# Second feed-forward layer of a hybrid decoder step: gate and up in seven block products

## The chip, the core and the metric

The kernel runs on one core of a Trainium2 chip. The metric is device time in microseconds (us) of one execution, the median of several runs. TensorE (PE) multiplies matrices out of SBUF into PSUM, VectorE (DVE) and ScalarE (ACT) work on both memories, GpSimd (POOL) on SBUF, and SP issues most DMAs. PE's weight loads are shown apart (PEld).

## What is computed

One inference step of a two-layer decoder trunk for 512 prompt tokens and 8 x 8 sample tokens, 576 columns in all: layer 0 is dilated attention, layer 1 an S5 state-space layer (SSM) with a gated output projection (GLU). A feed-forward layer follows each. Only the second feed-forward layer is changed:

```python
def rmsnorm(x, g):
    y = x * rsqrt(mean(x * x, -1) + 1e-6)
    return y * g

def swiglu(h, w_gate, w_up, w_down):          # 1024 -> 2816 -> 1024, float32
    return (silu(h @ w_gate) * (h @ w_up)) @ w_down

x = x + swiglu(rmsnorm(x, norm_ffn[1]), ffn_w_gate[1], ffn_w_up[1], ffn_w_down[1])
```

## The kernel before

Activations are held transposed in `xT`: 8 tiles of 128 features by 576 tokens, the tokens in two halves of 288 (`HN`), each half in a PSUM bank of its own. Float32 products are made of three rounded ones: every operand is split into a high part and the rest (`whi`/`wlo` for weights, `xgh`/`xgl` for activations, `hh`/`hl` for the hidden layer), and `mm6` (L105) issues high x high, high x rest and rest x high for both halves of the tokens, six matmuls of 128 x 288.

`ffn` (L1003) runs for both layers. The hidden width goes in three thirds of 4, 4 and 3 block columns of 256 (`THIRDS`). In a block column, `gemm` loads gate weights in two chunks of 512 KB, splits each (`split_w`, L96: `whi` by ScalarE at L99, `wlo` by VectorE at L100) and accumulates 96 matmuls into two of three rotating PSUM tiles (`acc`, two banks each). VectorE scales by `nin.r`, the inverse norm of each token (L1034), ScalarE takes silu (L1035), GpSimd scales again for the up factor (L1036). Then the same for up; VectorE multiplies (L1041) and the product is split into `hh` and `hl` (L173, L174). After a third, four down projections follow, each added to `xT` (L1057). The last third of the second layer also writes the outputs.

`fetch_w` (L85) issues a weight load on SP's queue into one of four `raw` buffers, and `pace(rate)` (L78) adds `rate` (`RF` = 0.72) to a credit; for each whole credit SP also issues one copy of an old cache to its output, DRAM to DRAM (`o_kv_s<-cache_kv_w`, up to 1020 KB). These copies depend on nothing.

`Norm` (L182) prepares a layer's input: `add(m)` splits feature tile m times its gain (L178, L179) and sums the squares on ScalarE and GpSimd (L193, L194); `finish` sums over the partitions with a matmul by ones (L199), and forms `rstd` on ScalarE and VectorE (L203 to L213). The products with gate and up use the unscaled split, so they can start before `rstd` is there. The GLU of the SSM phase (`glu`, L1564 on) calls `add` for two tiles after each of its four rounds (yt at L1610, xT at L1612).

A scheduler orders the instructions of each engine; each engine runs its own in that order, and an instruction that waits holds up those behind it. In the first layer a generator (`fill`) adds the set-up of the SSM phase between matmuls: its matrices go through DRAM scratch (`e_scr`, `w_scr`, `t_scr`, `v_scr`).

Of the kernel before, what the change touches and what calls it, by code (L numbers as in the profile page):

```python
# [18 lines left out]
D = 1024  # L19
# [13 lines left out]
KST = 6  # L33
RF = 0.72
CHUNKS = ((0, 2), (1, 2), (2, 2), (0, 1), (1, 1), (0, 0), (1, 0), (2, 0), (2, 1))
# [5 lines left out]
def dram(ap, off, dims):  # L41
    return bass.AP(tensor=ap.tensor, offset=ap.offset + off, ap=[list(d) for d in dims])
# [8 lines left out]
def _build(nc, tc, A, es):  # L51
# [100 lines left out]
    xT = xp.tile([128, KT, NT], F32, name="xT")  # L152
    xg = es.enter_context(pool("xg", bufs=8))
    accp = [es.enter_context(tc.tile_pool(name=f"acc2{i}", bufs=1, space=PSUM)) for i in range(3)]
# [8 lines left out]
    aux = es.enter_context(tc.tile_pool(name="aux2", bufs=1, space=PSUM))  # L163
    nrm = es.enter_context(pool("nrm"))
    scn = {"W": scr.tile([8, 128, 2, 4, 128], F32, name="w_scr"), "V": scr.tile([8, 2, 64, 4, 2, 128], F32, name="v_scr"),
# [16 lines left out]
    class Norm:  # L182
# [4 lines left out]
        def add(self, m):  # L187
            self.x[m] = split(self.xs, xT[:, m, :], gm[:, self.gi, m:m + 1], "xgh", "xgl", self.perm)
            if m == 0:
                s.activation(self.ss, xT[:, m, :], AF.Square)  # L190
            else:
                sq = nrm.tile([128, NT], F32, name="sq")
                s.activation(sq, xT[:, m, :], AF.Square)  # L193
                g.tensor_tensor(self.ss, self.ss, sq, OP.add)  # L194

        def finish(self):
# [15 lines left out]
            else:  # L212
                v.scalar_tensor_tensor(self.r, t, 1.5, self.r, op0=OP.add, op1=OP.mult)  # L213

    n0 = Norm(1)
    with ExitStack() as p3:
# [9 lines left out]
    n1 = Norm(2, perm=True)  # L226
    ffn(nc, tc, A, L, 0, n0, n1, ssm)
    n1.finish()
    with ExitStack() as p4:
        n2 = ssm_phase(nc, tc, A, p4, L, n1, sp)  # L230
    ecx.close()
    n2.finish()
    ffn(nc, tc, A, L, 1, n2, None, None)
    assert not shifts

# [766 lines left out]

def ffn(nc, tc, A, L, layer, nin, nout, fill):  # L1003
    v, s, g, te = nc.vector, nc.scalar, nc.gpsimd, nc.tensor
    ident, pool, xT, load_w, mm6, acc, aux = (L[x] for x in ("ident", "pool", "xT", "load_w", "mm6", "acc", "aux"))
    lw = lambda n: dram(A[n], layer * D * FF, [[1, D * FF]])

# [16 lines left out]
    with ExitStack() as es:  # L1024
        hp = es.enter_context(pool("hp", bufs=9))
        wk = es.enter_context(pool("wkf", bufs=2))
        for c0, c1 in THIRDS:
# [15 lines left out]
            for c in range(4):  # L1043
                ks = range(2 * c0, 2 * c1)
                done = c1 == 11 and nout is None
                if done and c == 3:
                    ps = [acc() for _ in range(3)]
                    ws = [load_w(lw("ffn_w_down"), D, k, min(4, 2 * c1 - k), c * 256, 256) for k in ks[::4]]
                else:
                    ps, ws = gemm(lw("ffn_w_down"), D, ks, c * 256, h), None  # L1050
                for m in range(2):
                    if ws is not None:
# [3 lines left out]
                    xv = xT[:, 2 * c + m, :].rearrange("p (a b) -> p a b", a=2)  # L1056
                    v.tensor_tensor(xv, ps[m][:, :, :HN], xv, OP.add)  # L1057
                    if c1 == 11 and nout is not None:
                        nout.add(2 * c + m)
                    if not done:  # L1060
                        continue
                    if m == 0 or c == 3:
                        w = 128 if c == 3 else 256
                        yo = wk.tile([128, 4, w], F32, name="yo")
                        ys = wk.tile([64, w], F32, name="ys")
# [11 lines left out]
        if fill is not None:  # L1077
            for _ in fill:
                pass

# [315 lines left out]
def ssm_phase(nc, tc, A, es, L, nin, sp):  # L1396
    v, s, g, te = nc.vector, nc.scalar, nc.gpsimd, nc.tensor
    ident, pool, xT, fetch_w, split_w, mm6, acc, aux, scn, xg = (L[x] for x in ("ident", "pool", "xT", "fetch_w", "split_w", "mm6", "acc", "aux", "scn", "xg"))
    Ar, Ai, E63, rho, x0, xs0, KC, consts_in, consts_out = (sp[x] for x in ("Ar", "Ai", "E63", "rho", "x0", "xs0", "KC", "consts_in", "consts_out"))
    wk = es.enter_context(pool("wks", bufs=2))  # L1400
    kp = es.enter_context(pool("kps"))
    zm = kp.tile([128, 64], F32, name="zm")
    g.memset(zm, 1.0)
# [19 lines left out]
    def stage1(c, mid=None, at=(1, 0)):  # L1423
# [12 lines left out]
        for m in range(2):  # L1436
            f = 2 * c + m
            u = wk.tile([128, 2, HN], F32, name="yt", bufs=2)
            v.tensor_tensor(u, ps[m][:, :, :HN], nin.r, OP.mult)
            nc.sync.dma_start(scn["U"][f], u.rearrange("p h x -> p (h x)"))  # L1440
# [91 lines left out]
    def states():  # L1532
# [8 lines left out]
        g.tensor_tensor(fs[:, 1], t1, t2, OP.add)  # L1541
        u12 = wk.tile([128, 2, 8, 32], F32, name="R", bufs=1)
        u1, u2 = u12[:, 0], u12[:, 1]
        a8r, a8i = (x[:, 8:9, :].to_broadcast([128, 8, 32]) for x in (Ar, Ai))
        for sgn, ri, (p, q) in ((OP.subtract, 0, ((a8r, x0[:, 0]), (a8i, x0[:, 1]))), (OP.add, 1, ((a8r, x0[:, 1]), (a8i, x0[:, 0])))):
# [3 lines left out]
            g.tensor_tensor(Ss[:, ri], Ss[:, ri], u1, OP.add)  # L1549
        fo = wk.tile([32, 128, 2], F32, name="fo", bufs=1)  # L1550
        so = wk.tile([128, 2, 128, 2], F32, name="ys")
        pt = aux.tile([128, 2, 512], F32, name="aux")
# [9 lines left out]
        nc.sync.dma_start(dram(A["o_st_s"], 0, [[256, 128], [32768, 2], [1, 256]]), so.rearrange("p h a r -> p h (a r)"))  # L1562

    def glu(c0):  # L1564
# [14 lines left out]
    def glu_first():  # L1579
# [5 lines left out]
        for m in range(2):  # L1585
# [3 lines left out]
            if m == 0:  # L1589
                stage3(7)  # L1590
        gsplit(4, ("ys", 7), ("Xt", 7))
        sp["es"].close()
        N[0] = L["Norm"](3, L["es"].enter_context(L["right"]("xg2", bufs=8)))
        w = [(ps, *split_w(W2[c0][1])) for ps, c0 in ((pg, D), (pv, 0))]
# [6 lines left out]
    for c in range(4):  # L1601
        pg, pv = glu_first() if c == 0 else (glu(D + c * 256), None)
        sg = []
        for m in range(2):
            t = wk.tile([128, 2, HN], F32, name="yt", bufs=2)
            s.activation(t, pg[m][:, :, :HN], AF.Sigmoid)
            sg.append(t)
# [59 lines left out]


# [14 lines left out]
```

## Time and profile before

| what | value |
|---|---|
| time, median of 3 runs | 1490.38 us (1488.93 to 1492.78) |
| span of the profiled execution | 1486.7 us |
| median less that span | 3.7 us |
| PE, PEld busy | 98%, 92% of the span |
| DVE, ACT, POOL busy | 60%, 35%, 23% |
| matmuls | 12662 |
| first feed-forward layer | about 401 to 870 us |
| SSM phase with GLU | about 870 to 1067 us |
| second feed-forward layer | about 1067 to 1487 us |

The page gives no time of its own for the profiled execution, only its span, from the first to the last instruction; what lies around it is in the medians. Rows of groups read: line, engine, operation, output<-inputs, shapes, count, then total busy us and mean ns of one, then the idle time before them and who ended it. Rows of stretches read: stretch, its length, then for PE, PEld, DVE, ACT and POOL the busy us and in brackets the instructions, then the granted clock of TensorE, the mean busy share of the DMA engines and GB/s. Rows of the chain of waits read: start, length, engine, tile, line. Rows of waits read: who waited for whom, us in total, times, longest. Rows of DMAs read: transfer, issuing queue, count, size, median us from issue to landing.

### The profile page before, as it was taken

Reading aid. Unit: us, or ns where it says so; the run is one execution under the profiler, and the core shown is the slowest. Engines: PE = TensorE matmul, PEld = TensorE weight load, DVE = VectorE, ACT = ScalarE, POOL = GpSimd, SP = SyncE. Lnnn points to the kernel's source line nnn. Section 1 sums busy time; section 2 is a strip of 40 time slices with the busy share of each in tenths; the row PEclk is TensorE's granted clock in tenths of the full one; section 3 lists DMA queues with packets and bytes.
Section 4 is the critical chain, followed back from the end, with each engine's and each line's share of the span. In section 5 each row is a group of like instructions: output and inputs, shape, how many; then the busy total and the mean of one; then the engine's idle time right before and its main releaser. Section 6 shows DMA issues by size and latency. Waiting matters only on the chain.

```text
span 1486.7 us, 30078 instructions
## 1 busy us (share of the span) xinstructions
PE 1457.7 (98%) x12662; PEld 1370.9 (92%) x12662; DVE 896.0 (60%) x1507; ACT 526.8 (35%) x814; POOL 335.4 (23%) x393
## 2 busy tenths in 40 slices
PE   9999999999999999999999999799999999999998
PEld 7888777777899999999999999699999999999998
DVE  6898989645669545778676668745433333333342
ACT  4534455465552211332223444333422222211222
POOL 2022232310030174354444321301111000100100
PEclk9999999999999999999999999899999999999999
DMA  7566698999885557687867748724475565544212
GB/s 248 205 238 234 230 304 268 361 302 348 246 289 184 205 177 247 229 300 266 283 225 259 267 129 267 219 91 140 156 252 179 192 223 197 197 166 138 85 56 82
DMA packets 191607, 322.66 MB, mean 217 GB/s; under 512 B 40017, under 2 KB 138129, under 8 KB 190065
## 3 DMA queue, kind: packets, MB, share of 16 engines
q1 hardware_dynamic: 183488, 303.24, 60.3%
q0 software_dynamic: 5216, 14.82, 2.9%
q10 hardware_dynamic: 2768, 2.70, 0.5%
q8 instruction: 99, 1.62, 0.4%
q14 instruction: 36, 0.29, 0.1%
HBM read 289.22 MB, written 118.78 MB: 274 GB/s over the span
## 4 chain that ended last, share of the span: by engine, by line
PE 85%; DVE 4%; DMA 4%; POOL 3%; issue 2%; ACT 2%; SPq 0%; ACTq 0%; DVEq 0%; POOLq 0%
PE acc L108 62%; PE acc L340 12%; PE Sd L767 2%; DMA kc<-cache_kv_w 1%; PE S L767 1%; PE O L767 1%; PE pt L573 1%; DMA U<-u_scr 1%; PE aux L108 1%; PE pt L767 1%; DVE u L767 1%; PE aux L1495 1%; DMA y_scr<-ys 1%; DMA e_scr<-ee 1%; DVE a L767 1%
## 5 line engine op out<-in xcount | busy, mean ns | idle before, releaser
L108 PE MATMUL acc<-xgh,whi 128*128 128x288 f32 x1760 | 379.5, 297 | 0.1
L108 PE MATMUL acc<-xgh,wlo 128*128 128x288 f32 x1760 | 375.9, 295 | 1.9 <-DVE wlo L100 1.9
L108 PE MATMUL acc<-xgl,whi 128*128 128x288 f32 x1760 | 377.5, 295 | 0.0
L100 DVE TENSOR_TENSOR wlo<-raw,whi 128x1024 fp32r<-128x1024 f32 (+1 forms) x166 | 209.2, 1260 | 232.6 <-ACT whi L99 229.1
L99 ACT ACTIVATE whi<-raw 128x1024 fp32r<-128x1024 f32 (+1 forms) x166 | 172.4, 1039 | 473.2 <-PE acc L108 422.1
L108 PEld LDWEIGHTS acc<-xgh,wlo 128*128 128x128 f32 x1760 | 282.6, 188 | 2.5 <-DVE wlo L100 2.3
L108 PEld LDWEIGHTS acc<-xgh,whi 128*128 128x128 f32 x1760 | 281.7, 188 | 2.1 <-issue 1.2
L108 PEld LDWEIGHTS acc<-xgl,whi 128*128 128x128 f32 x1760 | 282.6, 188 | 0.2
L1036 POOL TENSOR_TENSOR gt<-gt,rstd 128x576 f32<-128x576 f32 x44 | 76.7, 1744 | 486.6 <-ACT gt L1035 486.4
L108 PE MATMUL acc<-hh,whi 128*128 128x288 f32 x704 | 151.3, 296 | 0.0
L108 PE MATMUL acc<-hh,wlo 128*128 128x288 f32 x704 | 150.6, 295 | 0.0
L108 PE MATMUL acc<-hl,whi 128*128 128x288 f32 x704 | 150.6, 295 | 0.0
L340 PE MATMUL acc<-whi,xh 128*128 128x512 f32 x288 | 118.7, 414 | 2.0 <-ACT xh L280 1.8
L108 PEld LDWEIGHTS acc<-hh,whi 128*128 128x128 f32 x704 | 112.9, 188 | 0.4 <-issue 0.4
L108 PEld LDWEIGHTS acc<-hl,whi 128*128 128x128 f32 x704 | 113.0, 188 | 0.0
L108 PEld LDWEIGHTS acc<-hh,wlo 128*128 128x128 f32 x704 | 112.9, 188 | 0.0
L340 PE MATMUL acc<-wlo,xh 128*128 128x512 f32 x288 | 112.2, 391 | 0.0
L340 PE MATMUL acc<-whi,xl 128*128 128x512 f32 x288 | 111.5, 393 | 0.0
L194 POOL TENSOR_TENSOR ssum<-ssum,sq 128x576 f32<-128x576 f32 x21 | 36.2, 1725 | 152.5 <-ACT sq L193 123.0
L1057 DVE TENSOR_TENSOR xT<-acc,xT 128x576 f32<-128x576 f32 x48 | 36.3, 756 | 54.6 <-PE acc L108 54.6
L1035 ACT ACTIVATE gt<-gt 128x576 f32<-128x576 f32 x44 | 30.1, 685 | 100.7 <-DVE gt L1034 100.6
L340 PEld LDWEIGHTS acc<-whi,xh 128*128 128x128 f32 x288 | 54.0, 188 | 12.6 <-ACT xh L280 2.4
(399 smaller groups left out, 2022.8 us busy)
## 6 DMA issues: line engine op xcount, KB each, us to landing
o_kv_s<-cache_kv_w SPq DMA_DIRECT2D x64, 1020.0 KB, 6.9
kc<-cache_kv_w SPq DMA_DIRECT2D x100, 512.0 KB, 6.9
raw<-ffn_w_gate SPq DMA_DIRECT2D x44, 512.0 KB, 4.0
raw<-ffn_w_up SPq DMA_DIRECT2D x44, 512.0 KB, 3.9
raw<-ffn_w_down SPq DMA_DIRECT2D x40, 512.0 KB, 3.6
raw<-w_qkv SPq DMA_DIRECT2D x36, 512.0 KB, 6.9
kc<-qscr SPq DMA_DIRECT2D x32, 512.0 KB, 6.0
o_kv_s<-cache_kv_w SPq DMA_DIRECT2D x16, 1008.0 KB, 6.4
```

The source lines that it names most:

```text
L99: s.activation(hi, raw, AF.Copy)
L100: mark[0] = v.tensor_tensor(lo, raw, hi.bitcast(F32), OP.subtract)
L108: pem[0] = te.matmul(ps[:, c, :HN], w, x[:, c * HN:(c + 1) * HN], start=first and i == 0, stop=last and i == 2)
L194: g.tensor_tensor(self.ss, self.ss, sq, OP.add)
L340: ins = nc.tensor.matmul(*a, **kw)
L573: tc.keep_in_program_order(te.transpose(kp[:, hp, :], self.kc[u // 2][:, u % 2, hp * 128:(hp + 1) * 128], ident))
L767: return lambda *a, **kw: self.tc.keep_in_program_order(f(*a, **kw))
L1035: s.activation(t, t, AF.Silu)
L1036: g.tensor_tensor(t, t, nin.r, OP.mult)
L1057: v.tensor_tensor(xv, ps[m][:, :, :HN], xv, OP.add)
L1495: te.matmul(Y[h:h + 64, gl, q * 72:q * 72 + 72], w[:, h:h + 64], x, start=st, stop=not st)
```

## The change

The second layer gets a function of its own, `ffn_last`; `ffn` keeps the first. For each block column the gate and up weights are a matrix of 2 x 2 blocks: two halves of its columns (m) by feature tiles of even and odd number (k). The activations are 2 x 2 blocks too: even and odd tiles by the two token halves. Seven block products in Winograd's order replace eight:

- The host lays the weights out by blocks (`w_gu`), 512 KB each, every partition's 4 KB in one piece.
- `fetch` loads a11, a12 and a22 as they are, and a21 twice, as s1 and s3. **Adding DMAs** on GpSimd's queue (`plus`) add a22 to s1 and a11 to s3. VectorE forms s2 = s1 + a11 in the buffer `S2`, and when that is split, another adding DMA adds a12 to it: s4.
- `Norm7` forms the seven activation operands (b11, t1, b21, t2, t3, t4, b22), split, once per pair of tiles, in half widths.
- `unit` runs a block column. A product is 24 matmuls: 12 into bank 0 (gate), 12 into bank 1 (up). PSUM tile X takes a11, then s2, s3 and a22, which accumulate on each other; Y takes s1 and s4; Z takes a12. **Partial sums are read between**: a11 and s3 to `cp`, s2 to `cq`, Y after s3 has run. The matmuls stand in written order.
- The second scaling of gate stays on GpSimd in the last third alone; in the others the down result is scaled by `nin.r`.
- Splits use three buffer pairs instead of two. Gate and up loads no longer pace cache copies; `RF` is 1.0, so the first layer issues more of them.
- Some buffers of the SSM phase move so that the memory for this is free in time.

```diff
-RF = 0.72
+RF = 1.0
...
+    class Norm7(Norm):
...
+        def put(self, n, j, src, sc):
+            hi = self.xs.tile([128, HN], F32R, name="xoh")
+            lo = self.xs.tile([128, HN], F32R, name="xol")
+            s.activation(hi, src, AF.Copy, scale=sc)
+            v.scalar_tensor_tensor(lo, src, sc, hi.bitcast(F32), op0=OP.mult, op1=OP.subtract)
+            self.x[n, j] = hi, lo
...
+            self.put("b11", j, e0, ge)
+            s.activation(a, e1, AF.Copy, scale=ge)
+            v.scalar_tensor_tensor(b, e0, ge, a, op0=OP.mult, op1=OP.subtract)
+            self.put("t1", j, b, 1.0)
+            self.put("b21", j, o0, go)
+            v.scalar_tensor_tensor(c, o1, go, b, op0=OP.mult, op1=OP.add)
+            self.put("t2", j, c, -1.0)
...
+PRODUCTS = (("a11", "b11"), ("s1", "t1"), ("a12", "b21"), ("s2", "t2"), ("s3", "t3"), ("a22", "t4"), ("s4", "b22"))
...
+    def split_w(raw):
+        turn[0] += 1
+        p, n = (ring, "") if turn[0] % 3 else (r7, "3")
...
+    def plus(t, c, m, k):
+        g.dma_start(fl(t), block(c, m, k), accum_op=OP.add)
+
+    def fetch(c):
+        w = {"a11": load(c, 0, 0, ring, "raw", 4)}
+        for n, a in (("s1", (1, 1)), ("s3", (0, 0))):
+            w[n] = load(c, 1, 0, r7, n, 2)
+            plus(w[n], c, *a)
+        w["a12"] = load(c, 0, 1, ring, "raw", 4)
+        w["a22"] = load(c, 1, 1, ring, "raw", 4)
+        return w
...
+            bank = dict(a11=X, s1=Y, a12=Z, s2=X, s3=X, a22=X, s4=Y)
...
+                if n == "s2":
+                    w["s2"] = r7.tile([128, 4, 256], F32, name="S2")
+                    v.tensor_tensor(w["s2"], w["s1"], w["a11"], OP.add)
+                wh, wl = split_w(w[n])
+                if n == "s2":
+                    w["s4"] = w["s2"]
+                    plus(w["s4"], c, 0, 1)
+                if n == "s3" and c + 1 < 11:
+                    W[c + 1] = fetch(c + 1)
...
+                for i in range(2):
+                    for k in range(4):
+                        for j, (a, b) in enumerate(((wh, 0), (wh, 1), (wl, 0))):
+                            tc.keep_in_program_order(te.matmul(P[:, i, :HN], a[:, k, i * 128:(i + 1) * 128], nin.x[x, k][b],
...
+                    if n in ("a11", "s3"):
+                        s.activation(cp[0][i], p, AF.Copy)
+                    elif n == "a12":
+                        v.tensor_tensor(t[i][0][:, 0], p, cp[0][i], OP.add)
+                    elif n == "s2":
+                        s.activation(cp[1][i], p, AF.Copy)
+                    elif n == "a22":
+                        s.activation(t[i][1][:, 0], p, AF.Copy)
+                    elif n == "s4":
+                        v.tensor_tensor(t[i][0][:, 1], p, cp[1][i], OP.add)
+                    if n == "s3":
+                        v.tensor_tensor(t[i][1][:, 1], Y[:, i, :HN], cp[0][i], OP.add)
...
+                    if i == 0:
+                        v.scalar_tensor_tensor(sg[m], sg[m], sgn, nin.r, op0=OP.mult, op1=OP.mult)
+                        s.activation(sg[m], sg[m], AF.Silu)
+                        if scaled:
+                            g.tensor_tensor(sg[m], sg[m], nin.r, OP.mult)
+                    else:
+                        u = t[1][m]
+                        v.scalar_tensor_tensor(u, u, sgn, sg[m], op0=OP.mult, op1=OP.mult)
+                        h[2 * c + m] = L["split"](hp, u.rearrange("p a b -> p (a b)"), None, "hh", "hl")
```

Three places show what the scheduler made of it. The first is TensorE's queue where the GLU ends and the layer starts, first before (`acc_12519` is the gate's first PSUM tile in block column 0, `aux<-ssum,ones` the matmul with ones):

```order
L108 MATMUL acc_12519<-xgh,whi 128x288 x2
L108 MATMUL acc_12519<-xgl,whi 128x288 x2
L108 MATMUL acc_12519<-xgh,wlo 128x288 x2
L108 MATMUL acc_12519<-xgh,whi 128x288 x2
L199 MATMUL aux<-ssum,ones 128x288 x2
L108 MATMUL acc_12519<-xgl,whi 128x288 x2
L108 MATMUL acc_12519<-xgh,wlo 128x288 x2
```

and after (`acc_12480` is the GLU's last tile, `acc_12667` is X of block column 0):

```order
L108 MATMUL acc_12480<-xgh,whi 128x288 x2
L108 MATMUL acc_12480<-xgl,whi 128x288 x2
L108 MATMUL acc_12480<-xgh,wlo 128x288 x2
L203 MATMUL aux<-ssum,ones 128x288 x2
L1160 MATMUL acc_12667<-xoh,whi 128x288
L1160 MATMUL acc_12667<-xol,whi 128x288
```

The matmul with ones moved from among the gate's matmuls to a place behind the GLU's last and ahead of the layer's first matmul.

The second is ScalarE's queue in block column 1 of the changed kernel (numbers tell the buffers apart: `S2_13016` is split first as s2, later as s4; `raw_13053` and `s1_13055` belong to block column 2; cp, cq, gt1 and ut1 are read out of PSUM tile X, `acc0_12917`):

```order
L1108 ACTIVATE whi3_13049<-s3_12808 128x1024
L1108 ACTIVATE whi_13093<-raw_12813 128x1024
L1168 ACTIVATE cq0_12922<-acc0_12917 128x288
L1108 ACTIVATE whi_13130<-S2_13016 128x1024
L1168 ACTIVATE cq1_12923<-acc0_12917 128x288
L1164 ACTIVATE cp0_12920<-acc0_12917 128x288
L1108 ACTIVATE whi3_13178<-raw_13053 128x1024
L1164 ACTIVATE cp1_12921<-acc0_12917 128x288
L1170 ACTIVATE gt1_12925<-acc0_12917 128x288
L1181 ACTIVATE gt1_12925<-gt1_12925 128x576
L1108 ACTIVATE whi_13208<-s1_13055 128x1024
```

Where before the queue held one split and one silu or hh in turn, copies out of PSUM now stand between splits; the copy cq1 stands behind the split of s4.

The third is GpSimd's queue in the same part, adding DMAs alone:

```order
L1123 DMA s1_13055<-w_gu 128x1024
L1123 DMA S2_12766<-w_gu 128x1024
L1123 DMA s3_13058<-w_gu 128x1024
L1123 DMA s1_13305<-w_gu 128x1024
L1123 DMA S2_13016<-w_gu 128x1024
L1123 DMA s3_13308<-w_gu 128x1024
```

Each S2 of one block column stands between s1 and s3 of the column that is two further on.

More of the change, by code (lines that the diff above doesn't have):

```diff
@@ L213, in finish, with __init__, add @@
                 v.scalar_tensor_tensor(self.r, t, 1.5, self.r, op0=OP.add, op1=OP.mult)
+    class Norm7(Norm):
+        def __init__(self, gi, xo, tp):
+            super().__init__(gi, xo)
+            self.tp = tp
+        def put(self, n, j, src, sc):
[4 more added lines that the diff above has]
+            self.x[n, j] = hi, lo
+        def add(self, m):
+            if m % 2 == 0:
+                self.square(m)
+                return
+            j = m // 2
+            ge, go = (gm[:, self.gi, k:k + 1] for k in (m - 1, m))
+            e0, e1, o0, o1 = (xT[:, k, c * HN:(c + 1) * HN] for k in (m - 1, m) for c in range(2))
+            t = self.tp.tile([128, 1024], F32, name="S2")
+            a, b, c = (t[:, i * HN:(i + 1) * HN] for i in range(3))
+            self.put("b11", j, e0, ge)
[5 more added lines that the diff above has]
+            self.put("t2", j, c, -1.0)
+            v.scalar_tensor_tensor(a, o1, go, a, op0=OP.mult, op1=OP.subtract)
+            self.put("t3", j, a, 1.0)
+            v.scalar_tensor_tensor(b, o0, go, c, op0=OP.mult, op1=OP.subtract)
+            self.put("t4", j, b, -1.0)
+            self.put("b22", j, o1, go)
+            self.square(m)
     n0 = Norm(1)
@@ L1043, in ffn @@
             for c in range(4):
[L1044 to L1050, printed above, removed]
-                for m in range(2):
-                    if ws is not None:
+                ps = gemm(lw("ffn_w_down"), D, range(2 * c0, 2 * c1), c * 256, h)
```

119 lines of the change are left out of this document (97 added, 22 removed).

## The prediction

> **What bounds the kernel now.** I read the page first (two lines), then busy time by stretches of time, the chain of waits, and ScalarE's timeline inside the layer that is changed (two lines).
>
> ```profile
> span 1486.7 us, 30078 instructions
> PE 1457.7 (98%) x12662; PEld 1370.9 (92%) x12662; DVE 896.0 (60%) x1507; ACT 526.8 (35%) x814; POOL 335.4 (23%) x393
> 1100.00:1200.00 100.00, 100.00 (x763) 100.00 (x763) 35.95 (x38) 23.84 (x26) 6.90 (x5) 1.00 0.58 210
> 1075.13 376.04 PE acc L108 x2847
> 1109.60 1.06 ACT L99 ACTIVATE whi<-raw 128x1024 fp32r<-128x1024 f32 x1 [1.41 <-PE acc L108]
> ...
> 1115.94 1.06 ACT L99 ACTIVATE whi<-raw 128x1024 fp32r<-128x1024 f32 x1 [4.60 <-PE acc L108]
> ```
>
> TensorE is busy 98% of the span, and in a stretch of the second feed-forward layer it is busy all of it at granted clock 1.00, with VectorE at 36%, ScalarE at 24% and the DMA engines at 0.58. The chain there is one piece of TensorE. Each weight split (whi) is released when TensorE has used up 48 matmuls, and two of them start 6.34 us apart: 6.34 / 48 = 0.132 us for a matmul of 288 columns. So whatever removes matmuls here pays at once, as long as nothing else is late.
>
> **What the change removes.** Gate and up take 11 block columns x 2 x 8 x 2 x 3 x 2 = 2112 matmuls before; seven products of 24 are 168 for a block column, 1848 in all. 264 fewer x 0.132 = **-34.9 us**. One product then lasts 24 x 0.132 = 3.17 us, half of it (one PSUM bank) 1.59, a block column 22.2.
>
> **The start of the layer.** Before, the matmul with ones that sums the squares stands among the gate's matmuls. After, it stands ahead of a11, whose order is fixed, so TensorE stands still until GpSimd has added the last square.
>
> ```profile
> 1058.30 0.75 DVE L1610 TENSOR_TENSOR yt<-acc,yt 128x576 f32<-128x576 f32 x1
> ...
> 1060.68 1.30 DVE L1612 TENSOR_TENSOR xT<-xT,yt 128x576 f32<-128x576 f32 x1
> ...
> 1062.70 0.67 ACT L193 ACTIVATE sq<-xT 128x576 f32<-128x576 f32 x1
> ...
> 1063.45 1.49 POOL L194 TENSOR_TENSOR ssum<-ssum,sq 128x576 f32<-128x576 f32 x1 [3.78 <-ACT sq L193]
> ...
> 1066.52 1.13 PE L199 MATMUL aux<-ssum,ones 128*128 128x288 f32 x4
> ```
>
> After the GLU's last matmul: yt 0.75, one half-width difference 0.45 (priced below), xT 1.30, a half-width split 0.4 on ScalarE, the square 0.67, the addition 1.49, handovers 0.15: 5.2 us. The matmul with ones (1.13) is paid either way. **+5.2 us.** The operand sums of `Norm7` (7 splits and 4 combinations per pair of feature tiles on VectorE, about 11 x 0.45 = 5 us) lie beside the GLU's matmuls (192 for a pair, 25 us) and, for the last pair, beside this wait and the products a11 to a12.
>
> **Inside a block column.** Prices:
>
> ```profile
> L767 DVE TENSOR_TENSOR wlo<-raw,whi 128x1024 fp32r<-128x1024 f32 x34 | 41.6, 1223 | 2.8 <-ACT whi L767 2.5
> L213 DVE SCALAR_TENSOR_TENSOR rstd<-sq,rstd 128x576 f32<-128x576 f32 x2 | 1.5, 758 | 0.1
> L1057 DVE TENSOR_TENSOR xT<-acc,xT 128x576 f32<-128x576 f32 x48 | 36.3, 756 | 54.6 <-PE acc L108 54.6
> L1481 DVE TENSOR_TENSOR Xt<-R,ta 64x252 f32<-64x252 f32 x16 | 6.7, 416 | 0.6
> L1456 ACT ACTIVATE Sb<-acc 128x576 f32<-128x576 f32 x8 | 5.2, 646 | 4.9 <-PE acc L1454 4.4 <-ACT Xt L1466 0.2
> L767 ACT ACTIVATE P<-pt 128x256 f32<-128x256 f32 x48 | 16.4, 376 | 28.8 <-PE O L767 19.9 <-PE pt L767 8.8
> L1035 ACT ACTIVATE gt<-gt 128x576 f32<-128x576 f32 x44 | 30.1, 685 | 100.7 <-DVE gt L1034 100.6
> ```
>
> By width, 288 columns cost VectorE 0.45 us (between 0.416 and 0.756) and ScalarE 0.40 (between 0.376 and 0.646). VectorE then does 7 wlo and one S2 sum (8 x 1.22), six additions out of PSUM (6 x 0.45), two sg and two u (4 x 0.76) and two hl (2 x 0.76): 17.0 of 22.2 us. ScalarE: 7 x 1.06 + 8 x 0.40 + 4 x 0.69 = 13.4. Neither bounds by its sum; their order does.
>
> In that order ScalarE has to do whi of s4 ahead of cq1, the copy that must be out of X before s3's second half may write there. TensorE wants that at 12.69 + 1.59 = 14.3 us after a11's start. whi of s4 waits for two things: s2's end (12.7, handover 0.2) and the adding DMA that turns S2 into s4. With the first alone cq1 ends at 12.9 + 1.06 + 0.4 + 0.1 = 14.5, a wait of 0.2; the next such copy (cp1 of s3, behind whi of the next a11) costs 0.15: 0.35 us in each column in any case.
>
> The DMA starts when VectorE has done wlo of S2, and VectorE gets there late. Counted from the a11 of the column before, it comes to sg for m=1 at 18.9, after its reads of s3. Its run from there, with the ends: sg 19.7; silu and whi of the next s1 on ScalarE 21.6, wlo 22.9; u 23.65; gt0 24.1; sg 24.9; hl 25.65; ut0 26.1; u 26.9; wlo of the next a12 28.1; meanwhile hh, cp0 and whi of S2 on ScalarE 29.1; wlo of S2 30.35. The column before took 22.2 and its 0.35 to 0.4 of waits, so this is 7.75 after the column's own a11. The wait at cq1 is therefore 7.8 + landing + 1.06 + 0.4 + 0.1 - 14.3 = landing - 4.9.
>
> What an adding DMA of 512 KB takes to land no row shows. Nearest:
>
> ```profile
> Wc<-w_scr POOLq DMA_DIRECT2D x4, 512.0 KB, 4.3
> Tc<-t_scr POOLq DMA_DIRECT2D x4, 512.0 KB, 7.2
> Vc<-v_scr POOLq DMA_DIRECT2D x4, 512.0 KB, 8.1
> ...
> o_kv_s<-cache_kv_w SPq DMA_DIRECT2D x8, 1020.0 KB, 5.9
> raw<-ffn_w_down SPq DMA_DIRECT2D x11, 512.0 KB, 3.5
> ```
>
> Plain DMAs from GpSimd's queue take 4.3 us alone and 7.2 to 8.1 several at once; in the FFN stretch a copy of 1020 KB takes 5.9. An addition needs the old contents as well, twice the data, so I go by the 1020 KB row, **6.0 us**, rounded up since the s1 sum for two columns on is issued 3 us before; bounds 4.3 and 8.1.
>
> The Trainium skill ("Collectives: The Full Stack", The bandwidth ceiling) puts the price of a reducing DMA down to its two source reads and not to the addition. Its "DMA: Bandwidth & Descriptors" (Anatomy of one DMA, SWDGE) has about 2.0 us plus the bytes at 436 GB/s; for 1 MB that makes an estimate of 4.4 us, by which the sum would be that of the first rival below. The rows lie above this line already (4.3 for 512 KB), and they decide here.
>
> Columns 1, 2, 3, 5, 6, 7: (6.0 - 4.9) + 0.15 = 1.25 each, 7.5. Columns 4 and 8 follow a down phase, where VectorE isn't late: 0.35 each, 0.7. Column 0: its s1 and S2 sums stand behind a load that waits for the S2 addition; a11 starts 6.4 after the GLU's end, wlo of S2 ends at 16.4, the landing at 22.5, cq1 at 24.1 against 21.2: 2.9. Columns 9 and 10 also wait for the scaling on GpSimd that remains in the last third:
>
> ```profile
> L1036 POOL TENSOR_TENSOR gt<-gt,rstd 128x576 f32<-128x576 f32 x44 | 76.7, 1744 | 486.6 <-ACT gt L1035 486.4
> ```
>
> some 1.4 of its 1.7 us are added to the run on VectorE: 2.65 each, 5.3. Together **+16.4 us**.
>
> A rule of the Trainium skill speaks against the layout itself: "Perfetto Trace Analysis" (Optimizing Tensor Performance, Matmuls) wants independent groups to rotate through PSUM banks so that evacuation overlaps the next matmuls; here s2, s3 and a22 follow each other in X. By the rule alone two handovers with two copies of 0.40 each would stand open, 11 x 1.6 = 18 us. The halves of X lie in two banks and 1.59 us of matmuls cover a copy of 0.40, so I count the queue in front of the copy and not the copy.
>
> **Down phases.** In the first two thirds three of the four raw buffers hold the next column's a11, a12 and a22, so all eight down loads go through one: load 3.5, whi 1.06, wlo 1.22, handovers 0.2 make 6.0 us against 6.34 that TensorE takes. Not bounding, but ScalarE's second whi waits for its load ahead of ut1, and the last hl arrives about 0.6 us late; in the last third the scaling does the same, about 0.4. **+1.5 us**, from 0 to 4 if loads take a microsecond more.
>
> **The first layer.** With RF 1.0 SP issues 20 copies of 1020 KB more before the first layer ends (20 stand in the second layer after, 40 before): 20.4 MB over 469 us, 43 GB/s.
>
> ```profile
> 525.00:591.00 66.00, 65.25 (x490) 65.01 (x488) 30.58 (x37) 11.31 (x11) 42.80 (x64) 1.00 0.65 218
> PE acc L108 <- DVE wlo L100: 1.7, 1, 1.7
> 574.18 8.73 DMA e_scr<-ee
> 584.28 2.19 DVE wt L1140
> 590.67 1.23 DVE wlo L100
> ```
>
> TensorE waits once in that layer, 1.7 us at 590, at the end of the SSM set-up, and the store e_scr (8.73) is on that chain. With 43 GB/s beside 218 it takes a fifth longer: **+2 us**, from 0 to 6 (three such stores).
>
> **Sum.** -34.9 + 5.2 + 16.4 + 1.5 + 2 = -9.8 us. The profiled span is 1486.7, 3.7 below the median of 1490.4 (2.2 to 6.1 below the three runs); the same difference stays: a span of 1477 and a time of **1480.6**. About 0.3%, 4.5 us, can be told from no change.
>
> **Rivals.** *The adding DMAs land like plain ones* (4.3): column 0 costs 1.2, columns 9 and 10 0.95 each, the others 0.35, 5.9 instead of 16.4, and with the smaller ends of the last two terms 1490.4 - 34.9 + 5.2 + 5.9 = 1467. For it: the calm DMA share (0.58), and blocks that come in rows of 4 KB. Against: the second read.
>
> *The landing decides, and the kernel is slower.* Nine columns pay each further microsecond, so from 6.0 + 9.8 / 9 = 7.1 on nothing is gained, and from 7.6 it is slower by more than can be doubted. At 8.1, the row of several at once, +9.1: 1499 or 1500; with the dearer ends of the down phases and the first layer (6.5 more) 1506. For it: three adding DMAs and five loads per 22 us, and sums queued behind each other. Against: their average spacing of 7 us.
>
> *The first layer eats it*: set-up stores late at several places, 8 us instead of 2, down phases 4: 1489, no change.
>
> *The change doesn't save what it says*: one bank takes 12 matmuls running, where before two alternated. If each of the 1848 became 10 ns longer, +18 us: 1499. For it nothing in the rows, since none shows such a run of 288 columns.
>
> **How the numbers follow.** Forecast 0.42, plain landing 0.20, late landing 0.22, first layer 0.10, longer matmuls 0.06. Faster: 0.36 of the forecast's 0.42 and all of the plain landing, 0.56. No change: 0.06 of the forecast, 0.08 of the first layer and 0.02 of the late landing, 0.16. Slower: the rest, 0.28. The likeliest time is 1480.6. The range goes from the plain landing, 1466, to the late landing with dear ends, 1506, and leaves out less than 0.2; the forecast's own is 1473 to 1487.
>
> **What would show it.** In the profile after: TensorE with 264 matmuls fewer; one idle piece of about 5 us before the matmul with ones; per column an idle piece of 1 us or so in the middle, ended by ScalarE's cq, and ahead of it whi of s4 waiting for a DMA on GpSimd's queue. The landing time of that DMA is the number to look up first: below 5 the first rival holds, above 7 the second. It would all be wrong if matmuls were longer than 0.132 us, or if TensorE waited mostly for wlo, which would say that VectorE's 17 us are the bound.

## The result, and the profile after

The changed kernel takes 1580.51 us (1578.90 to 1583.21), the kernel before 1491.14 us in the same comparison: a ratio of 1.0589 (1.0563 to 1.0615), 89 us slower. The forecast was 1480.6 us with a range from 1466 to 1506.

The page of the changed kernel, its first two lines, and the same stretch of the second feed-forward layer as shown of before:

```profile
span 1577.1 us, 30037 instructions
PE 1456.6 (92%) x12398; PEld 1348.2 (85%) x12398; DVE 1002.3 (64%) x1669; ACT 600.3 (38%) x959; POOL 333.7 (21%) x410
1100.00:1200.00 100.00, 77.67 (x531) 72.28 (x530) 49.80 (x61) 40.23 (x59) 7.79 (x9) 0.98 0.58 150
```

The 264 matmuls are gone (12398 instead of 12662), but TensorE is busy for only 77.67 of 100 us where it was busy for all of it. No other engine is near its limit: VectorE 49.8, ScalarE 40.2 of 100. So TensorE waits for something that is neither work nor bandwidth. The group of the product's first matmuls says for whom (its last part is the idle time ahead of them, and who ended it):

```profile
L1160 PE MATMUL acc<-xoh,whi 128*128 128x288 f32 x616 | 191.5, 311 | 78.1 <-ACT cp L1164 28.0 <-ACT cq L1168 19.9 <-DVE gt L1172 14.0
```

78.1 us of waits for the reads of PSUM: `cp`, `cq`, `gt`. A **handover** below is such a place: a group of matmuls that starts only when a read of partial sums has ended. TensorE's timeline shows their pattern. These are the rows with a wait between the middle of a12 in block column 1 and the same place in column 2:

```profile
1118.05 0.40 PE L1160 MATMUL acc<-xoh,whi 128*128 128x288 f32 x1 [1.06 <-DVE gt L1166]
1121.99 0.41 PE L1160 MATMUL acc<-xoh,whi 128*128 128x288 f32 x1 [0.50 <-ACT cq L1168]
1125.17 0.40 PE L1160 MATMUL acc<-xoh,whi 128*128 128x288 f32 x1 [1.31 <-ACT cq L1168]
1127.53 0.40 PE L1160 MATMUL acc<-xoh,whi 128*128 128x288 f32 x1 [0.50 <-ACT cp L1164]
1130.75 0.40 PE L1160 MATMUL acc<-xoh,whi 128*128 128x288 f32 x1 [1.36 <-ACT cp L1164]
1133.11 0.40 PE L1160 MATMUL acc<-xoh,whi 128*128 128x288 f32 x1 [0.50 <-ACT gt L1170]
1138.28 0.40 PE L1160 MATMUL acc<-xoh,whi 128*128 128x288 f32 x1 [1.73 <-DVE gt L1172]
1142.55 0.40 PE L1160 MATMUL acc<-xoh,whi 128*128 128x288 f32 x1 [0.83 <-ACT cp L1164]
1150.23 0.40 PE L1160 MATMUL acc<-xoh,whi 128*128 128x288 f32 x1 [1.05 <-DVE gt L1166]
```

A block column lasts 1150.23 - 1118.05 = 32.2 us instead of 22.2, and has eight waits in it. From 1118.05 on stand 24 matmuls, a12's second half and s2's first: 24 x 0.132 = 3.17, yet 3.94 us pass until 1121.99. The wait there stands between the first and the second half of s2, which go to different banks of X. ScalarE's rows about the second and third wait:

```profile
1121.53 0.41 ACT L1168 ACTIVATE cq<-acc 128x288 f32<-128x288 f32 x1 [0.66 <-PE acc L1160]
1123.76 1.06 ACT L1108 ACTIVATE whi<-S 128x1024 fp32r<-128x1024 f32 x1 [1.82 <-PE acc L1160]
1124.72 0.39 ACT L1168 ACTIVATE cq<-acc 128x288 f32<-128x288 f32 x1
```

The copy cq0 starts when s2's first half is done, and the second half starts at 1121.99, when cq0 has ended (1121.94). The second copy stands behind whi of s4, as the prediction had it, but that split waits for TensorE and not for a DMA. Where no split stands ahead, a handover so costs 3.94 - 3.17 = 0.77 us: 0.31 until the copy starts, 0.41 for the copy, 0.05 until TensorE goes on. The profile counts 0.50 of these as idle, and 0.27 lie under the modelled end of the last matmul. The profile lists 81 such waits in the layer.

### The profile page after: what moved, and what is told of

It is laid out like the page before. It is cut to its first block, busy times and chain, and to the rows that moved or that the text cites. A ratio compares the mean times of both kernels' runs of the same rounds, so it can differ in the third digit from the quotient of the medians.

```text
span 1577.1 us, 30037 instructions
## 1 busy us (share of the span) xinstructions
PE 1456.6 (92%) x12398; PEld 1348.2 (85%) x12398; DVE 1002.3 (64%) x1669; ACT 600.3 (38%) x959; POOL 333.7 (21%) x410
## 3 DMA queue, kind: packets, MB, share of 16 engines
q8 instruction: 97, 1.59, 0.4%
## 4 chain that ended last, share of the span: by engine, by line
PE 77%; DVE 6%; ACT 6%; issue 4%; DMA 4%; POOL 3%; SPq 0%; ACTq 0%; DVEq 0%; POOLq 0%
PE acc L108 41%; PE acc L1160 14%; PE acc L380 12%; ACT whi L1108 2%; PE Sd L807 2%; DMA kc<-cache_kv_w 1%; PE O L807 1%; PE S L807 1%; PE pt L613 1%; DMA U<-u_scr 1%; PE aux L108 1%; ACT cp L1164 1%; DVE ut L1186 1%; DVE wlo L1109 1%; PE pt L807 1%
## 5 line engine op out<-in xcount | busy, mean ns | idle before, releaser
L1160 PE MATMUL acc<-xoh,whi 128*128 128x288 f32 x616 | 191.5, 311 | 78.1 <-ACT cp L1164 28.0
L108 PE MATMUL acc<-xgh,wlo 128*128 128x288 f32 x1056 | 227.7, 297 | 3.8 <-DVE wlo L100 3.8
L108 PE MATMUL acc<-xgh,whi 128*128 128x288 f32 x1056 | 229.7, 299 | 0.0
L108 PE MATMUL acc<-xgl,whi 128*128 128x288 f32 x1056 | 227.5, 297 | 0.0
L1160 PE MATMUL acc<-xol,whi 128*128 128x288 f32 x616 | 182.9, 297 | 0.0
L1160 PE MATMUL acc<-xoh,wlo 128*128 128x288 f32 x616 | 182.7, 297 | 0.0
L100 DVE TENSOR_TENSOR wlo<-raw,whi 128x1024 fp32r<-128x1024 f32 x98 | 125.8, 1283 | 67.2 <-ACT whi L99 65.9
L1109 DVE TENSOR_TENSOR wlo<-raw,whi 128x1024 fp32r<-128x1024 f32 (+1 forms) x57 | 67.7, 1188 | 93.0 <-ACT whi L1108 92.9
L1160 PEld LDWEIGHTS acc<-xol,whi 128*128 128x128 f32 x616 | 117.0, 190 | 0.1
L1160 PEld LDWEIGHTS acc<-xoh,wlo 128*128 128x128 f32 x616 | 117.1, 190 | 0.0
```

Source lines behind the costliest of these rows:

```text
L100: mark[0] = v.tensor_tensor(lo, raw, hi.bitcast(F32), OP.subtract)
L108: pem[0] = te.matmul(ps[:, c, :HN], w, x[:, c * HN:(c + 1) * HN], start=first and i == 0, stop=last and i == 2)
L1109: v.tensor_tensor(lo, raw, hi.bitcast(F32), OP.subtract)
L1160: tc.keep_in_program_order(te.matmul(P[:, i, :HN], a[:, k, i * 128:(i + 1) * 128], nin.x[x, k][b], skip_group_check=n not in ("a12",), sta ...
```

## The experiments

**Theory A (tile):** the program makes matmuls into one bank of a PSUM tile wait for a read of the tile's other bank, since its waits go by tile. (What puts the wait there, the scheduler or a later step, no run here shows.) **Rival B (queue):** the copies are late because splits stand ahead of them. **Rival C (PSUM):** the chip does not let TensorE run while another engine reads PSUM.

### One tile for each bank (six_tiles)

```diff
-            X, Y, Z = (accp[i].tile([128, 2, 512], F32, name=f"acc{i}") for i in range(3))
+            X, Y, Z = ([hb[i][c].tile([128, 512], F32, name=f"acc{i}{c}") for c in range(2)] for i in range(3))
...
-te.matmul(P[:, i, :HN], ...)
+te.matmul(P[i][:, :HN], ...)
```

> X, Y and Z of the second layer become two PSUM tiles of one bank each, nothing else. Theory A (one tile): a block column lasts 32.2 us instead of 22.2 since matmuls of one half wait until the copy or sum has read the other half of the same PSUM tile, eight such handovers in a column, 7.8 us of idle time and 0.27 us of pipeline end for each. Then they go, the column falls to about 23.7 with the queue terms of the prediction, and the time to 1580.5 - 11 x 8.5 = 1487 (1475 to 1500). Rival B (queue): the copies are late because ScalarE and VectorE do splits ahead of them; then it stays at 1570 to 1580. Rival C (PSUM): TensorE cannot run while another engine reads its PSUM; then it stays within 5 us of 1580 as well.

Measured: 1483.58 us, 0.9939 of the kernel before (0.9918 to 0.9959). The tiles of the down projections are split the same way, their sums are read by halves, and the pool of the small PSUM tile (`aux`) is opened ahead of the others. The same group of matmuls in this kernel, and ScalarE's rows of a column about the places shown above:

```profile
L1176 PE MATMUL acc<-xoh,whi 128*128 128x288 f32 x616 | 184.0, 299 | 8.5 <-ACT cq L1184 7.9 <-DVE gt L1232 0.5
...
1115.52 0.41 ACT L1184 ACTIVATE cq<-acc 128x288 f32<-128x288 f32 x1 [0.61 <-PE acc L1176]
1116.98 1.06 ACT L1110 ACTIVATE whi<-S 128x1024 fp32r<-128x1024 f32 x1 [1.05 <-PE acc L1176]
1117.94 0.39 ACT L1184 ACTIVATE cq<-acc 128x288 f32<-128x288 f32 x1
```

78.1 us of idle time became 8.5 without a change in what is computed. The second cq still stands behind the split of s4, so the queue there is the old one; and from 1108 to 1140, while ScalarE reads PSUM ten times, TensorE does not wait once. A holds; B and C, which left the time near 1580, are out.

### ScalarE in written order (order_two_bank, six_order)

```diff
-        s.activation(hi, raw, AF.Copy)
+        tc.keep_in_program_order(s.activation(hi, raw, AF.Copy))
...
+                P = bank[n]
+                if q + 1 < 7:
+                    nxt = prep(PRODUCTS[q + 1][0])
```

The copies out of PSUM are held in the same way. The first has the two-bank tiles, the second the one-bank tiles.

> The two-bank tiles stay; the splits are written one product earlier and ScalarE is held to the written order, so that every copy out of X stands ahead of the next split. Theory A: the eight handovers stay and only what lay behind a split goes, 0.8 + 0.9 + 0.3 = 2.0 us in a column: 1580.5 - 22 = 1558 (1550 to 1565). Rival B (queue): all waits for ScalarE go, about 6 us in a column: 1515 or less. Rival C: as A.

> One-bank tiles and ScalarE in the order of order_two_bank together. Theory A: the column falls to nearly 22.2, since neither a tile nor a split stands before a copy: 5 to 15 us below six_tiles, 1470 to 1482. Rival B: as order_two_bank, since the tiles change nothing. Rival D (VectorE or the landing of the adding DMAs is the next bound): no better than six_tiles, with TensorE waiting for wlo.

Measured: 1607.03 us (1.0773 of the kernel before, 1.0752 to 1.0795) and 1554.65 us (1.0428, 1.0412 to 1.0443). The first is outside every expectation, the second meets only Rival D's, no better than six_tiles. For order_two_bank TensorE's rows of a column, and then the groups:

```profile
1124.05 0.41 PE L1171 MATMUL acc<-xoh,whi 128*128 128x288 f32 x1 [0.50 <-ACT cq L1179]
1126.41 0.40 PE L1171 MATMUL acc<-xoh,whi 128*128 128x288 f32 x1 [0.50 <-ACT cq L1179]
1154.90 0.40 PE L1171 MATMUL acc<-xoh,whi 128*128 128x288 f32 x1 [0.50 <-ACT cq L1179]
```

```profile
L1171 PE MATMUL acc<-xoh,whi 128*128 128x288 f32 x616 | 193.1, 314 | 67.4 <-ACT cp L1175 27.0 <-DVE gt L1177 11.7 <-ACT cq L1179 11.0
...
L108 PE MATMUL acc<-hh,whi 128*128 128x288 f32 x352 | 82.1, 317 | 17.8 <-ACT whi L1108 17.8
```

In five of the eight handovers of this column ScalarE is idle when its copy falls due, and each of them still has its 0.50 of idle time. Two belong to VectorE, and one, a11's first copy, again stands behind a split (1.60). A column is 1154.90 - 1124.05 = 30.85 us, 1.3 shorter than in the changed kernel and not 6. That is A and not B. The total says nothing here, since the held order also bound other splits: TensorE waits 17.8 us for those of the down projections instead of about 3, and 5.1 us at the start of the layer.

The same holds for six_order, 71 us above six_tiles; its groups with idle time:

```profile
L1187 PE MATMUL acc<-xoh,wlo 128*128 128x288 f32 x616 | 190.0, 308 | 14.7 <-DVE wlo L1111 14.7
L1187 PE MATMUL acc<-xoh,whi 128*128 128x288 f32 x616 | 189.0, 307 | 15.7 <-ACT whi L1110 15.2 <-DVE gt L1243 0.5
...
L1151 PE MATMUL acc<-hh,whi 128*128 128x288 f32 x352 | 81.7, 315 | 20.6 <-ACT whi L1110 20.6
```

No wait for a copy is left, but 50 us of waits for splits that the written order holds back: the scheduler's order of ScalarE, which I had blamed in part, was the better one. Rival D's sign (TensorE waits for wlo) appears. I put it down to the order and not to VectorE's load; no run separates the two.

### Reads written behind both halves, two-bank tiles (late_reads)

```diff
-                    p = P[:, i, :HN]
+                for i in range(2):
+                    p = P[:, i, :HN]
```

> The two-bank tiles of the changed kernel stay, but every read of a partial sum is written behind all 24 matmuls of its product instead of behind each half. Theory A (waits go by tile): of eight handovers in a column two are left, from s2 to s3 and from s3 to a22, and each costs two copies and the pipeline's end, 1.2 us, or 2.2 where a split stands ahead: 2.4 to 4.4 us in a column instead of 10, 1580.5 - 11 x 5.6 to 7.6 = 1497 to 1519, although no copy starts earlier than before and most start later. If early reads were good for the time, as the prediction took it (1.59 us of matmuls cover a copy), it is slower than 1580.

Measured: 1536.25 us in two runs (1530.09 and 1542.41), 44 us less than the changed kernel, although no read is written earlier and most are written later. The two runs lie 12 us apart, so the size is rough.

```profile
L1160 PE MATMUL acc<-xoh,whi 128*128 128x288 f32 x616 | 190.7, 310 | 42.8 <-ACT cq L1169 28.3 <-ACT cp L1165 14.5
```

The sign is A's; the size is less than I expected, since the two handovers left cost 1.6 us of idle time, and from 1.8 to 4.9 where cq also waits for the split of s4. That split waits for the DMA into S2 here (7 times, 24.9 us of ScalarE's time): the prediction's own wait, which the long column of the changed kernel had hidden.

### The same wait in the kernel before (before_between, before_behind)

The kernel before with its eight products; in the second layer gate and up are written by token halves, and VectorE's reads stand between the halves or behind both (`BETWEEN` is true in the first and false in the second; shortened):

```diff
+        for c in range(2):
+            for k in range(4):
+                for i, (w, x) in enumerate(((wh, xh), (wh, xl), (wl, xh))):
+                    te.matmul(p[:, c, :HN], w[:, k], x[:, c * HN:(c + 1) * HN], ...)
+            if last and BETWEEN:
+                rd(p, c)
+        if last and not BETWEEN:
+            for c in range(2):
+                rd(p, c)
```

> The kernel before, eight products as ever, but in the second layer gate and up are written by token halves: 48 matmuls into one bank of a tile, VectorE's read of it, then 48 into the other bank. Theory A (waits go by tile): 44 tiles with one handover each, 0.8 to 1.6 us (0.45 to read, up to a split of 1.2 ahead of it on VectorE, 0.3 the pipeline's end), 35 to 70 us, and about 9 at the start of the layer, since the written order leaves the matmul with ones in front: 1535 to 1570. If the cause lies in the seven products and not in the tile: as before_behind.

> The same matmuls in the same order as before_between, but both halves of a tile are read behind all 96 matmuls. Theory A: no handover is left, since the next tile is another one: the kernel before plus the 9 us at the start of the layer, 1500 (1494 to 1506).

Measured: 1548.70 and 1501.54 us. The matmuls' groups of the one and the other:

```profile
L1017 PE MATMUL acc<-xgh,whi 128*128 128x288 f32 x704 | 212.6, 302 | 35.3 <-DVE gt L1047 18.0 <-DVE ut L1061 17.3
```

```profile
L1017 PE MATMUL acc<-xgh,whi 128*128 128x288 f32 x704 | 209.2, 297 | 0.0
```

Same matmuls, same order; only the place of one read in each of 44 tiles differs, and it costs 47.2 us, 1.07 a tile. So the cost belongs to the read between two halves of one tile and not to the seven products. The other 10 us of before_behind (1501.5 against 1491.5) are the start of the layer, with the matmul with ones in front: TensorE waits 7.1 us for it, and it takes 2.29 us instead of 1.13.

### The start of the layer (six_late_ones, six_late_b)

```diff
-    n2.finish()
...
+                if c == 0 and n == "s2":
+                    nin.finish()
```

> One-bank tiles, and the matmul with ones and the inverse norm are written behind a12 of block column 0 instead of ahead of the layer. In the changed kernel TensorE stood still 6.6 us for the last square, the matmul with ones took 1.2 us longer and twelve matmuls ran at 0.24 instead of 0.132 us, 9 us in all. If that place is the cause, a wait of about 3 us for the last split of a11's operand is left and the time is 5 to 7 us below six_tiles. If the operand sums of the last pair of tiles are what is late, it is 0 to 2 us below.

> As six_late_ones, with the pool of the small PSUM tile opened behind the others again, as in the changed kernel. The three kernels with one-bank tiles reached the output projection 4 us later than the changed kernel did, ahead of everything that was edited on purpose. If the moved pool is the cause: 4 us below six_late_ones, 1469.5. If not: 1473.

Measured: 1473.36 us (0.9876 of before, 0.9859 to 0.9892) and 1473.27 us (0.9866, 0.9847 to 0.9884). The place of the matmul with ones is worth 10 us, more than the 5 to 7 expected. TensorE's rows in six_late_ones show where they come from:

```profile
1068.43 0.37 PE L1177 MATMUL acc<-xoh,whi 128*128 128x288 f32 x1 [2.35 <-ACT whi L1109]
...
1079.58 1.13 PE L204 MATMUL aux<-ssum,ones 128*128 128x288 f32 x4
...
1085.17 0.40 PE L1177 MATMUL acc<-xoh,whi 128*128 128x288 f32 x1 [1.29 <-ACT cq L1185]
```

The wait at the start falls from 6.6 to 2.35 us, now for the split of a11's weights, and the matmul with ones takes 1.13 instead of 2.29. Not foreseen was that the wait at cq in column 0 shrinks too, from the 5.37 of six_tiles to 1.29 and another 0.39. The slower clock behind the wait at the start, however, stays in this kernel (last section).

Opening the small pool last gains nothing in the total. The profile of six_late_b does reach the output projection as early as the changed kernel (395.4 us both, six_late_ones 399.4), and then waits more in the second layer. But two kernels with the same code up to that place differ as much (394.3 in the kernel before, 398.3 in before_between), so the 4 us that this run was made for cannot be told from the spread between executions.

### The cache copies (before_rf1, six_late_b_rf)

The first is the kernel before with `RF = 1.0`. The second is six_late_b with `RF = 0.72` and a copy issued for seven in ten of the loads of a11, a12 and a22.

> The kernel before with the rate of cache copies at 1.0 and nothing else. The prediction's term for the first layer is +2 (0 to 6): 1492 to 1493. The profile of the changed kernel has its GLU end 5 us later than before: if the copies are all of that, 1496. If they are free, 1491.

> As six_late_b, with the first layer's cache copies back at the rate of the kernel before (0.72), and the copies that are left issued beside the block loads of the second layer. If the copies are what made the first layer and the SSM phase longer (2 us by the prediction, 5 us by the profile of the changed kernel up to the end of the GLU): 2 to 5 us below six_late_b, unless the copies in the second layer make the adding DMAs land later, which costs up to a microsecond in each of some columns: then 0 to 6 us above.

Measured: 1492.81 us (1.0007, 0.9997 to 1.0016) and 1494.83 us (1.0015, 1.0000 to 1.0030). In the first layer the copies cost about 1 us, which cannot be told from nothing; the longest wait there grows from 1.7 to 2.4 us. The row of waits of before_rf1 (us in total, times, longest):

```profile
PE acc L108 <- DVE wlo L100: 2.6, 2, 2.4
```

In the second layer they cost 1494.83 - 1473.27 = 21.6 us. Adding DMAs into S2, first in six_late_b, then in six_late_b_rf, and the group of matmuls of the latter:

```profile
S<-w_gu POOLq DMA_DIRECT2D x11, 512.0 KB, 5.9
```

```profile
S<-w_gu POOLq DMA_DIRECT2D x11, 512.0 KB, 9.2
```

```profile
L1180 PE MATMUL acc<-xoh,whi 128*128 128x288 f32 x616 | 186.1, 302 | 26.1 <-ACT cq L1188 22.7 <-ACT cp L1184 2.9 <-DVE gt L1236 0.5
```

### s4 by VectorE (six_late_dve, six_late_dve_rf)

```diff
-                    plus(w["s4"], c, 0, 1)
+                    v.tensor_tensor(w["s4"], w["s2"], w["a12"], OP.add)
```

> As six_late_b, but s4 is formed by VectorE (S2 + a12, 1.22 us in each column, VectorE is busy 60% there) instead of an adding DMA, so no landing stands ahead of cq1. In six_late_b about 4 us of idle time at cq1 and the slower clock behind it are left: 1468 to 1472 if they go. If VectorE's queue becomes the bound, TensorE waits for wlo and the time is 1475 to 1490.

> As six_late_dve, with the copies of six_late_b_rf (0.72 in the first layer, the rest beside the block loads), which made that kernel 1494.8 us, with S2's adding DMA landing after 9.2 us instead of 5.9. Theory E (what the copies hurt is the landing of s4, which cq1 waits for): the 21 us go, 1468 to 1475. Rival F (the copies delay the plain loads or the sums s1 and s3, or TensorE through the traffic): 1485 to 1495 as before.

Measured: 1468.87 us (0.9844, 0.9823 to 0.9864), the best of all, and 1471.29 us (0.9879, 0.9855 to 0.9903). With the copies in the second layer (six_late_dve_rf), the adding DMAs that are left and the group of matmuls:

```profile
s<-w_gu POOLq DMA_DIRECT2D x22, 512.0 KB, 7.3
```

```profile
L1180 PE MATMUL acc<-xoh,whi 128*128 128x288 f32 x616 | 182.9, 297 | 2.3 <-ACT cq L1188 1.8 <-DVE gt L1236 0.5
```

The other adding DMAs land after 7.3 us, and TensorE has no wait in the block columns that six_late_dve, without the copies, lacks; the idle time at cq falls from 22.7 to 1.8. So what the copies hurt was the one landing in front of cq1 (Theory E), not the loads or TensorE.

## Why the prediction was wrong, step by step

**The step that failed** is this one: "The halves of X lie in two banks and 1.59 us of matmuls cover a copy of 0.40, so I count the queue in front of the copy and not the copy." The matmuls of the second half do not run beside the copy: they wait for it. (The sentence speaks of X; for the halves of Y and Z I took the same without saying so.) I read the banks off the kernel's code and took it that a wait follows the bank; in this program it follows the tile. In the kernel before nothing could show it, since `mm6` writes both halves in turn and every read comes behind both, so its feed-forward layers have no matmul beside a read of its own tile. That should have made the cover an unknown with two ends, none of it to all of it. With none of it, eight handovers of 0.4 for the copy and 0.3 for the pipeline's end would have been 8 x 11 x 0.7 = 62 us, outside my range on the slow side. None of my rivals named this mechanism.

The Trainium skill ("Perfetto Trace Analysis", Optimizing Tensor Performance, Matmuls) wants groups to rotate through banks. I weighed it, at two open handovers and 18 us, and set it aside. By its direction it was right; the price is for eight handovers a column, since each half of a product is handed over by itself. The Trainium skill's page "PSUM — Partial Sum Buffer" (PSUM bank collisions raise a hardware error) keeps engines apart by bank. six_tiles agrees with that: with a tile for each bank copies and matmuls of neighbouring banks run together, 8.5 us of waits in place of 78.1.

**The other terms**, for the changed kernel's span of 1577.1 against 1486.7:

| term | predicted | measured |
|---|---|---|
| 264 matmuls fewer | -34.9 | -34.9 (12 matmuls still take 1.59) |
| start of the layer | +5.2 | about +9 |
| block columns | +16.4 | about +100 (78 idle and 81 x 0.27) |
| down phases | +1.5 | about +7 |
| up to the GLU's end | +2 | +5, of which the copies 1 |

The rows leave some 4 of the 90 us without a place. The 0.27 was worked out at one handover and is an estimate for the others.

*Start of the layer.* The wait was foreseen, its length less so. The matmul with ones after, and ahead of it VectorE's rows:

```profile
1063.71 1.34 DVE L228 SCALAR_TENSOR_TENSOR xol<-xT,gm,xoh 128x288 fp32r<-128x288 f32 x1 [1.24 <-ACT xoh L227]
1064.97 0.74 DVE L1772 TENSOR_TENSOR yt<-acc,yt 128x576 f32<-128x576 f32 x1
...
1070.06 2.29 PE L203 MATMUL aux<-ssum,ones 128*128 128x288 f32 x4 [6.59 <-POOL ssum L198]
```

The GLU ends at 1070.06 - 6.59 = 1063.5, and yt starts 1.5 us later behind an operand's split (xol, 1.34): what I had laid "beside the GLU's matmuls" was partly still queued. That makes 6.6 instead of 5.2; the rest is the slower clock, below.

*Block columns in six_tiles*, where the prediction's mechanism can act: it put 16.4 us there, and 8.5 of idle time were found, 5.4 of them in column 0. There the prediction has 2.9, though its own figures give 3.4: a11 starts at 6.4 and cq1 is wanted 14.3 later, at 20.7 and not at 21.2.

```profile
1094.09 0.61 PE L1176 MATMUL acc<-xoh,whi 128*128 128x288 f32 x1 [5.37 <-ACT cq L1184]
...
1282.50 0.41 PE L1176 MATMUL acc<-xoh,whi 128*128 128x288 f32 x1 [0.39 <-ACT cq L1184]
...
1294.93 1.23 DVE L1111 TENSOR_TENSOR wlo<-S,whi 128x1024 fp32r<-128x1024 f32 x1 [0.59 <-ACT whi L1110]
```

The landing was sized well (6.0 predicted, 6.1 in six_tiles, 5.9 in six_late_b). VectorE was less late: the row at 1282.50 is the start of s3's second half, 60 matmuls ahead of the next a11, which so starts at 1290.5; wlo of S2 ends at 1296.2, 5.7 later and not 7.75. So a landing of 6 us is mostly covered. The mechanism itself was right, as six_late_b_rf shows: with a landing of 9.2 us it costs 21.6 us. That six_tiles came out at 1483.6, close to the forecast, is in part luck, since the start of the layer cost more and the columns less.

*Down phases.* In the changed kernel TensorE waits eight times in them, 5.2 us in all and some 0.27 more for each; the longest, 1.06 us, stand at the start of a phase and end with a late split. In six_tiles the corresponding group has 0.3 us, so this was mostly a consequence of the same waits.

*The first layer.* +2 predicted, 1 measured in before_rf1 (-0.4 to 2.4 by the interval). That the changed kernel is 5 us late at the GLU's end is therefore not the copies alone. Part of it can be the spread between executions: the GLU's first sum (yt) starts at 979.1 us in the kernel before and at 983.7 in the changed one, but also at 980.9 and 983.5 in before_behind and before_between, which have the code of the kernel before up to there. How much of the 5 us the change itself costs stays open.

*Rivals.* Longer matmuls: out, 0.132 as before. Plain landing: the landing was 5.4 us in the changed kernel and 5.9 to 6.1 with one-bank tiles, not 4.3. Late landing: its mechanism exists (six_late_b_rf), but in the changed kernel a column of 32 us hid it. First layer: out, the copies cost it about 1 us.

## What to carry to other kernels

A read of a partial sum between two groups of matmuls is only free if the program lets the next matmuls start; look in the order of the instructions for what each first matmul of a group waits, before counting its neighbours as cover. Here two banks in one tile meant one wait for both, and a tile for each bank turned 1580 us into 1484. Where the trace of before has no row in which two things overlap, their overlap is an unknown with two ends, not a fact of the layout.

A chain with one DMA in it (split, landing, split, copy) fails by the traffic beside it: take the DMA out of the chain (here for an addition of 1.22 us in each column on VectorE, which is then busy for 41 of the 55 us from 1100 to 1155 in six_late_dve), and the same traffic costs 2 us instead of 22.

## What the runs showed of the hardware

A pause of TensorE can cost more than its length. The stretches behind the wait at the start of the layer in the changed kernel (the granted clock is the third number from the end):

```profile
1065.00:1070.00 5.00, 0.00 (x0) 0.00 (x0) 5.00 (x7) 1.60 (x4) 1.53 (x1) 0.84 0.00 0
1070.00:1072.00 2.00, 1.95 (x5) 1.51 (x5) 2.00 (x6) 1.24 (x4) 0.00 (x1) 0.50 0.00 0
1072.00:1075.00 3.00, 3.00 (x13) 2.74 (x11) 2.68 (x5) 2.95 (x5) 0.00 (x0) 0.50 0.00 0
1075.00:1078.00 3.00, 1.32 (x9) 1.10 (x9) 1.66 (x3) 1.84 (x3) 0.00 (x0) 0.96 0.82 310
```

The mean of 0.84 in the first row means that the clock fell from 1.00 to 0.50 at about 1068.4, 4.9 us after the GLU's end; by the last row it rose at about 1075.2. So it stood at 0.50 for 6.8 us, 5.2 of them with work: the matmul with ones took 2.29 instead of 1.13 us, and 12 matmuls 0.24 each instead of 0.132, 2.5 us in all. A wait of 2.35 us was enough in six_late_ones:

```profile
1068.00:1069.00 1.00, 0.57 (x3) 0.60 (x4) 1.00 (x3) 0.21 (x1) 0.00 (x0) 0.85 0.00 0
1072.00:1073.00 1.00, 1.00 (x9) 1.00 (x9) 1.00 (x2) 0.00 (x0) 0.70 (x1) 0.94 0.06 16
```

There the clock is at 0.50 from 1068.7 to 1072.1, 3.4 us, and the first matmuls of a11 take 0.24 each. The Trainium skill ("TensorE: Matmul & The Clock Gate", Part 1: The HAM clock gate) has the clock fall to half after an idle window of about 3.4 us, and rise after as long a busy one. The slow stretches of 3.4 and 6.8 us agree with such a window; that a whole idle one is needed does not agree with the fall after 2.35 us. The prediction left the clock out of the start of the layer.

An adding DMA takes longer to land than a plain load of the same blocks. The changed kernel's DMAs (the last number is the median from issue to landing):

```profile
raw<-w_gu SPq DMA_DIRECT2D x33, 512.0 KB, 3.3
...
s<-w_gu POOLq DMA_DIRECT2D x22, 512.0 KB, 6.5
...
S<-w_gu POOLq DMA_DIRECT2D x11, 512.0 KB, 5.4
```

It took 5.4 to 6.5 us against 3.3. The plain loads are issued from SP's queue and the adding ones from GpSimd's, and no run separates the addition from the queue. Into S2 it took 9.2 us with cache copies beside it (six_late_b_rf), but also 9.3 without them in six_order, so the copies are not the only thing that lengthens it.
